# Streaming rows at 192 bytes into a block of 256: a change of SBUF places in a two-block model kernel

## The chip, the core and the metric

The kernel runs on one core of one Trainium2 chip. A core has TensorE (PE: matrix products into PSUM, with its weight loads listed apart as PEld), VectorE (DVE), ScalarE (ACT), GpSimd (POOL) and SyncE (SP, here the queue of the weight transfers), which share the on-chip memory SBUF of 128 partitions. The metric is device time in microseconds (us) of one execution; the times are of three runs, and one further execution was profiled.

## The reference, cut to what matters

Two model blocks are computed one after the other on 256 tokens and 16 meta tokens (T = 272 rows), in float32. The first is a mixer (state-space part and convolution) followed by PEER, a layer that picks 16 experts per head for each token:

```python
q = (xt @ w_query).reshape(t, PEER_HEADS, PEER_DKEY)
v1, i1 = lax.top_k(s1, PEER_TOPK)       # s1, s2: q against 128 sub-keys
...
act = jax.nn.gelu(jnp.einsum("td,thkd->thk", xb, u), approximate=False) * gb
return jnp.einsum("thk,thkd->td", act, v)
```

The second has two layers, each with a SwiGLU feed-forward (FFN), an attention, an output projection and another FFN:

```python
h = h + 0.5 * _swiglu(_rms_norm(h, ln_ffn1[layer]), ffn1_wi[layer], ffn1_wo[layer])
hn = _rms_norm(h, ln_mix[layer])
...
h = h + mix @ w_out[layer]
h = h + 0.5 * _swiglu(_rms_norm(h, ln_ffn2[layer]), ffn2_wi[layer], ffn2_wo[layer])
```

## The kernel before

**Products.** The state `h` lies transposed: 8 tiles (KD) of 128 features, each with 272 token columns. All large products go through `mm3`. A float32 value is split into a high part (fp32r, made by ACT) and the rest (made by DVE or POOL), for the weights (`wH`, `wL`, `_split`) and for the data (`uH`, `uL` and others, `hilo`). Each 128x128 weight tile then gives three matmuls, wH with xH, wH with xL, wL with xH. The weight tile is the stationary operand; the data row, 256 or 272 columns of one feature tile, streams. These streaming rows are what the change moves.

**Weights.** `_load` fetches 8 weight tiles (512 KB) at a time on SP's queue into one of three `raw` buffers. `_split` makes halves of 4 tiles into one of five `wH` and `wL` buffers. A split of `wL` is DVE's, except for the share that `self.share` hands to POOL.

**Stages, in order.** `mixer`; `peer`; then `second`: FFN1, attention A (`attn_a`), FFN2, FFN3, attention B (`attn_b`), FFN4. Every FFN has a first part, 44 output tiles of 8 products-of-three with `uH`/`uL` (its pairs), and a second part of 8 tiles of 22 products-of-three with the gate rows `gH`/`gL`. FFN4 and the output projection of attention B work on 256 columns, `peer` too; FFN1 to FFN3 and attention A on 272.

**PEER.** First 16 query tiles; then 128 value rows r, each one output tile (24 matmuls) followed by a Gelu (L957, L960). Meanwhile `route` finds the top 16 on DVE. From r = 60 on, each row carries one group g of four tokens: `onehot(g)` on DVE (L931) compares the 128 key numbers with the chosen ones (`sel`), for both halves of an expert number at once; every fourth group is multiplied by its gate values on DVE (L933), the others by four ACT instructions (L936); `gates(g)` multiplies the halves on PE (L943), and DVE and ACT write the result into `buf` (L945, L947). `onehot` writes one of two buffers, so it runs a group ahead. After the 128 rows, PE runs the `up` products: for each of 128 gate rows, split into `uH`/`uL` by `act`, 24 matmuls at L999.

**Places.** `uH` and `uL` are each one tile of 8 rows of 272 columns. A row is 1088 bytes, so the starts of successive rows step by 64 within a block of 256 bytes. A pass over columns 16 to 271 (`self.u(M, T)`) begins 64 bytes later in each row. The gate rows of the FFNs have a pitch of 512 columns (256 in FFN4), behind a filler tile `gpad`.

Of the kernel before, what the change touches and what calls it, by code (L numbers as in the profile page):

```python
# [8 lines left out]
F32 = mybir.dt.float32  # L9
# [9 lines left out]
P = 128  # L19
# [20 lines left out]
R0 = 271  # L40
RW = 400
# [166 lines left out]
class Net:  # L208
    def __init__(self, tc, ctx, I, out, dump=None):
# [29 lines left out]
        self.uH = per.tile([P, KD, T], F32R, name="uH")  # L239
        self.uL = per.tile([P, KD, T], F32R, name="uL")  # L240
# [139 lines left out]
    def u(self, a=0, b=T):  # L380
        return lambda k: (self.uH[:, k, a:b], self.uL[:, k, a:b])
# [5 lines left out]
    def norm_tile(self, d):  # L387
        nc, a, b = self.nc, self.na, self.nb
        src = self.h[:, d, a:b]
        self.hilo(self.uH[:, d, a:b], self.uL[:, d, a:b], src, self.vec(self.nw, d))  # L390
# [58 lines left out]
    def mixer(self):  # L449
        nc = self.nc  # L450
        h = self.h
        with ExitStack() as ctx:
# [8 lines left out]
            yH, yL = self.uH[:, :, M:], self.uL[:, :, M:]  # L461
# [5 lines left out]
            nH = pool.tile([P, KD, T], F32R, name="nH")  # L467
            nL = pool.tile([P, KD, T], F32R, name="nL")
# [152 lines left out]
            pool = ctx.enter_context(self.tc.tile_pool(name="my", bufs=1))  # L621
            cH = pool.tile([P, KD, S], F32R, name="cH")
# [173 lines left out]
    def peer(self):  # L796
# [5 lines left out]
        with ExitStack() as ctx:  # L802
# [3 lines left out]
            sel = pool.tile([P, S, 2], F32, name="sel")  # L806
            gsel = pool.tile([P, S], F32, name="gsel")
# [37 lines left out]
            self.linear(16, KD, self.u(M, T), S, qf)  # L845
            nc.scalar.dma_start(out=hd_, in_=h[:, :, M:])
            for d in range(KD):
                t = self.t_("t", 2)[:, :S]
                nc.vector.scalar_tensor_tensor(out=t, in0=h[:, d, M:], scalar=self.vec("norm_ffn", d), in1=r, op0=ALU.mult, op1=ALU.mult)
                self.hilo(self.uH[:, d, M:], self.uL[:, d, M:], t)  # L850
# [18 lines left out]
            def route(tt):  # L869
# [51 lines left out]
                nc.vector.tensor_copy(out=sel[:, ts].rearrange("p t i -> p i t"), in_=p2[:, :256].rearrange("p (i t) -> p i t", i=2))  # L921
# [42 lines left out]
            for r_ in range(NT):  # L964
                self.linear(1, KD, self.u(M, T), S, lambda m, ps: value(r_, ps))
# [60 lines left out]
            def u(d):  # L1026
                self.hilo(self.uH[:, d, M:], self.uL[:, d, M:], h[:, d, M:], w2[:, d : d + 1])
# [37 lines left out]
    def ffn(self, nxt, final=False, lo=0, each=None):  # L1065
        nc = self.nc
        with self.tc.tile_pool(name="ff", bufs=1) as pool:
# [3 lines left out]
            pool.tile([P, 112], F32, name="gpad")  # L1071
# [64 lines left out]
    def attn_a(self, nxt):  # L1136
        nc = self.nc
        with ExitStack() as ctx:
# [70 lines left out]
            oH = pool.tile([P, 8, T], F32R, name="oH")  # L1209
            oL = pool.tile([P, 8, T], F32R, name="oL")  # L1210
# [111 lines left out]
    def attn_b(self, nxt):  # L1322
        nc = self.nc
        with ExitStack() as ctx:
# [5 lines left out]
            qH = pool.tile([P, 2, T], F32R, name="qH")  # L1330
            qL = pool.tile([P, 2, T], F32R, name="qL")
# [3 lines left out]
            vt = pool.tile([P, 3, 1024], F32, name="vt")  # L1335
            oH = pool.tile([P, 8, S], F32R, name="oH")
# [173 lines left out]
    def second(self):  # L1510
        self.share = 0.0
        with self.tc.tile_pool(name="bp", bufs=1) as bp:
# [7 lines left out]
            with self.psum(3, 2, 3):  # L1520
                for l in range(2):
                    if l:
                        self.ffn("ln_mix_1")
# [5 lines left out]
                    self.ffn(None if l else "ln_ffn1_1", final=(l == 1), lo=M * l)  # L1529
# [57 lines left out]
```

## Time and profile before

| | before |
|---|---|
| median of 3 runs | 2240.27 us (2238.11 to 2245.38) |
| profiled execution, its own time | 2239.97 us |
| span of the profile, first to last instruction | 2238.0 us |
| PE busy, matmuls | 2169.0 us, 97% of the span, 17351 |
| DVE, ACT, POOL busy | 1590.4, 1323.0, 671.7 us |
| transfers | 356.59 MB, 159 GB/s |

A matmul's duration in the profile is that of one in a pipeline, about 0.28 us, while the next one starts some 0.12 us later. How fast PE goes through a stage is therefore read from the number of matmuls in a stretch of time, or from the distance of two starts, not from durations or from the busy share.

### The profile page before, as it was taken

Reading aid. Unit: us, or ns where it says so; the run is one execution under the profiler, and the core shown is the slowest. Engines: PE = TensorE matmul, PEld = TensorE weight load, DVE = VectorE, ACT = ScalarE, POOL = GpSimd, SP = SyncE. Lnnn points to the kernel's source line nnn. Section 1 sums busy time; section 2 is a strip of 40 time slices with the busy share of each in tenths; the row PEclk is TensorE's granted clock in tenths of the full one; section 3 lists DMA queues with packets and bytes.
Section 4 is the critical chain, followed back from the end, with each engine's and each line's share of the span. In section 5 each row is a group of like instructions: output and inputs, shape, how many; then the busy total and the mean of one; then the engine's idle time right before and its main releaser. Section 6 shows DMA issues by size and latency. Waiting matters only on the chain.

```text
span 2238.0 us, 45779 instructions
## 1 busy us (share of the span) xinstructions
PE 2169.0 (97%) x17351; PEld 2096.4 (94%) x17351; DVE 1590.4 (71%) x3143; ACT 1323.0 (59%) x2857; POOL 671.7 (30%) x567
## 2 busy tenths in 40 slices
PE   8998998899999999999999999999999999899999
PEld 7987998899999999999999998899999999679999
DVE  8889789955778766666586655876656666877664
ACT  8776654556766755555565555765555555666553
POOL 6684744444555400000031114122201211512220
PEclk9999999999999999999999999999999999999999
DMA  4523644454444555555565554145555555204555
GB/s 170 166 97 133 201 148 142 154 186 151 142 136 139 181 189 188 186 184 188 186 207 188 179 168 144 58 150 173 178 179 170 177 174 187 76 29 128 192 183 169
DMA packets 103948, 356.59 MB, mean 159 GB/s; under 512 B 12416, under 2 KB 20016, under 8 KB 103344
## 3 DMA queue, kind: packets, MB, share of 16 engines
q1 hardware_dynamic: 100096, 346.06, 46.8%
q10 hardware_dynamic: 3632, 7.62, 1.1%
q8 instruction: 136, 2.23, 0.4%
q14 instruction: 84, 0.69, 0.1%
HBM read 351.51 MB, written 5.40 MB: 159 GB/s over the span
## 4 chain that ended last, share of the span: by engine, by line
PE 76%; DVE 14%; ACT 5%; issue 3%; POOL 1%; DMA 1%; DVEq 0%; SPq 0%; ACTq 0%; POOLq 0%
PE acc L999 16%; PE mm L317 13%; PE mm L315 13%; PE mm L316 13%; PE acc L317 4%; PE acc L315 4%; PE acc L316 4%; DVE wL L294 3%; DVE h L931 2%; ACT h L936 1%; ACT wH L288 1%; DVE acc L526 1%; PE mm L1461 1%; PE acc L1485 1%; PE acc L943 1%
## 5 line engine op out<-in xcount | busy, mean ns | idle before, releaser
L288 ACT ACTIVATE wH<-raw 128x512 fp32r<-128x512 f32 x1296 | 806.6, 628 | 559.9 <-PE mm L316 237.8
L294 DVE TENSOR_TENSOR wL<-raw,wH 128x512 fp32r<-128x512 f32 x1037 | 756.3, 731 | 381.0 <-ACT wH L288 358.7
L317 PE MATMUL mm<-uH,wL 128*128 128x256 f32 (+1 forms) x2168 | 620.1, 286 | 19.9 <-DVE wL L294 19.2
L315 PE MATMUL mm<-uH,wH 128*128 128x256 f32 (+1 forms) x2168 | 628.3, 290 | 9.9 <-ACT wH L288 7.0
L316 PE MATMUL mm<-uL,wH 128*128 128x256 f32 (+1 forms) x2168 | 618.9, 286 | 2.4 <-DVE uL L359 2.3
L294 POOL TENSOR_TENSOR wL<-raw,wH 128x512 fp32r<-128x512 f32 x259 | 383.4, 1485 | 462.9 <-ACT wH L288 354.0
L317 PEld LDWEIGHTS mm<-uH,wL 128*128 128x128 f32 x2168 | 411.0, 190 | 24.7 <-DVE wL L294 23.8
L315 PEld LDWEIGHTS mm<-uH,wH 128*128 128x128 f32 x2168 | 410.9, 190 | 15.5 <-ACT wH L288 8.7
L316 PEld LDWEIGHTS mm<-uL,wH 128*128 128x128 f32 x2168 | 410.7, 189 | 5.9 <-DVE uL L359 4.2
L999 PE MATMUL acc<-uH,wH 128*128 128x256 f32 x1024 | 288.4, 282 | 1.7 <-DVE h L1033 1.1
L999 PE MATMUL acc<-uL,wH 128*128 128x256 f32 x1024 | 287.7, 281 | 0.4 <-DVE uL L357 0.4
L999 PE MATMUL acc<-uH,wL 128*128 128x256 f32 x1024 | 287.2, 281 | 0.0
L1086 POOL TENSOR_TENSOR t<-t,g 128x272 f32<-128x272 f32 (+1 forms) x88 | 108.2, 1231 | 415.6 <-ACT wH L288 326.2
L317 PE MATMUL acc<-uH,wL 128*128 128x272 f32 (+1 forms) x728 | 209.4, 288 | 0.0
L315 PE MATMUL acc<-uH,wH 128*128 128x272 f32 (+1 forms) x728 | 209.1, 287 | 0.0
L316 PE MATMUL acc<-uL,wH 128*128 128x272 f32 (+1 forms) x728 | 208.7, 287 | 0.0
L317 PE MATMUL mm<-gH,wL 128*128 128x272 f32 (+1 forms) x704 | 199.9, 284 | 0.0
L315 PE MATMUL mm<-gH,wH 128*128 128x272 f32 (+1 forms) x704 | 199.9, 284 | 0.0
L316 PE MATMUL mm<-gL,wH 128*128 128x272 f32 (+1 forms) x704 | 199.8, 284 | 0.0
L999 PEld LDWEIGHTS acc<-uH,wH 128*128 128x128 f32 x1024 | 194.1, 190 | 2.5 <-DVE h L1033 1.5
L999 PEld LDWEIGHTS acc<-uL,wH 128*128 128x128 f32 x1024 | 193.1, 189 | 0.6 <-DVE uL L357 0.6
L999 PEld LDWEIGHTS acc<-uH,wL 128*128 128x128 f32 x1024 | 193.0, 189 | 0.0
(400 smaller groups left out, 3918.0 us busy)
## 6 DMA issues: line engine op xcount, KB each, us to landing
raw<-in_wall_dram SPq DMA_DIRECT2D x648, 512.0 KB, 3.3
bdram<-brow ACTq DMA_DIRECT2D x1, 3200.0 KB, 13.7
b<-bdram SPq DMA_DIRECT2D x8, 272.0 KB, 4.6
b<-bdram SPq DMA_DIRECT2D x8, 144.0 KB, 4.2
buf<-in_keys_dram ACTq DMA_DIRECT2D x1, 1024.0 KB, 6.4
hd<-h ACTq DMA_DIRECT2D x1, 1024.0 KB, 5.4
h<-hd ACTq DMA_DIRECT2D x1, 1024.0 KB, 6.4
uv<-in_uv_dram ACTq DMA_DIRECT2D x1, 1024.0 KB, 5.8
```

The costliest lines, as they stand in the source:

```text
L288: nc.scalar.activation(out=H, in_=w, func=AF.Copy)
L294: eng.tensor_tensor(out=L, in0=w, in1=H.bitcast(F32), op=ALU.subtract)
L315: mm(ps, H, xH, start=(k == 0), stop=False)
L316: mm(ps, H, xL, start=False, stop=False)
L317: mm(ps, L, xH, start=False, stop=(k == kt - 1))
L526: nc.vector.scalar_tensor_tensor(out=acc, in0=src, scalar=w, in1=acc, op0=ALU.mult, op1=ALU.add)
L931: nc.vector.tensor_tensor(out=o, in0=self.iota[:, None, None, :].to_broadcast([P, 4, 2, P]), in1=sel[:, ts, :, None].to_broadcast([P, 4, 2 ...
L936: nc.scalar.activation(out=o[:, t, 0], in_=o[:, t, 0], func=AF.Copy, scale=gsel[:, 4 * g + t : 4 * g + t + 1])
L943: nc.tensor.matmul(ps[:, :, t], o[:, t, 1], o[:, t, 0], start=True, stop=True)
L999: nc.tensor.matmul(o, a, b, start=(r == 0 and d % 2 == 0 and i == 0), stop=(r == NT - 1 and i == 2), skip_group_check=True)
L1086: nc.gpsimd.tensor_tensor(out=t, in0=t, in1=s, op=ALU.mult)
L1461: nc.tensor.matmul(ps[:, :nk], qa[hh][:, k, a : a + n], ckv[:, k, :nk], start=(k == 0), stop=(k == 1))
```

## The change

It gives places in SBUF to the rows that stream. In the diff (cut):

```diff
+PITCH = 320
+AT = 64
+NPAD = 64
+OPAD = 80
+QPAD = 112
+EPAD = 112
+GPADS = (336, 432, 400, 432)
...
-        self.uH = per.tile([P, KD, T], F32R, name="uH")
-        self.uL = per.tile([P, KD, T], F32R, name="uL")
+        per.tile([P, 48], F32, name="upad")
+        u = [per.tile([P, KD * PITCH], F32R, name=n) for n in ("uH", "uL")]
+        per.tile([P, 80], F32, name="wpad")
+        self.uH, self.uL = (t.rearrange("p (k c) -> p k c", c=PITCH) for t in u)
+        self.vH, self.vL = (t[:, : KD * S].rearrange("p (k c) -> p k c", c=S) for t in u)
...
     def u(self, a=0, b=T):
+        if a == M and b == T:
+            return lambda k: (self.vH[:, k], self.vL[:, k])
         return lambda k: (self.uH[:, k, a:b], self.uL[:, k, a:b])
...
-            nH = pool.tile([P, KD, T], F32R, name="nH")
-            nL = pool.tile([P, KD, T], F32R, name="nL")
+            pool.tile([P, NPAD], F32, name="npad")
+            nH = pool.tile([P, KD, PITCH], F32R, name="nH")[:, :, :T]
+            nL = pool.tile([P, KD, PITCH], F32R, name="nL")[:, :, :T]
...
+            pool.tile([P, 112], F32, name="cpad")
             cH = pool.tile([P, KD, S], F32R, name="cH")
...
-            sel = pool.tile([P, S, 2], F32, name="sel")
-            gsel = pool.tile([P, S], F32, name="gsel")
+            sel = [self.t_("g", 2)[:, :S] for _ in range(2)]
+            gsel = self.t_("ssq", 2)[:, :S]
...
-                nc.vector.tensor_tensor(out=o, in0=self.iota[:, None, None, :].to_broadcast([P, 4, 2, P]), in1=sel[:, ts, :, None].to_broadcast([P, 4, 2, P]), op=ALU.is_equal)
+                for i in range(2):
+                    nc.vector.tensor_tensor(out=o[:, :, i], in0=self.iota[:, None, :].to_broadcast([P, 4, P]), in1=sel[i][:, ts, None].to_broadcast([P, 4, P]), op=ALU.is_equal)
...
-                t = self.uH[:, i, M:], self.uL[:, i, M:]
+                t = self.uH[:, i, AT:], self.uL[:, i, AT:]
...
-            pool.tile([P, 112], F32, name="gpad")
+            pool.tile([P, pad], F32, name="gpad")
...
+            pool.tile([P, EPAD], F32, name="epad")
             oH = pool.tile([P, 8, S], F32R, name="oH")
```

`oH`/`oL` of attention A and `qH`/`qL` of attention B get a filler and the pitch of 320 columns in the same way as `nH`. The tables `sel` and `gsel`, which had tiles of their own, move into scratch buffers, which makes room.

The addresses of the two built programs give these places (bytes into a block of 256 at which the rows that stream start; "all" means 0, 64, 128 and 192 in turn). Weight tiles start at a multiple of 512 in both programs.

| rows, columns | matmuls | place before | place after | from a high row to its low row, modulo 1024: before, after |
|---|---|---|---|---|
| u, 272 | 3984 | all | 192 | 512, 0 |
| u in queries, values, w_out of the mixer, FFN4, 256 | 4704 | all | 192 | 512, 0 |
| u at L999, 256 | 3072 | one of the four for 24 matmuls | 192 | 512, 0 |
| n (mixer), 272 and 256 | 696 and 192 | all and all | 192 and 0 | 512, 0 |
| o of attention A, q of attention B, 272 | 192 and 216 | all | 192 | 512 (o), 128 (q); 0 |
| c (mixer), 256 | 192 | 192 | 128 | 0, 0 |
| o of attention B, 256 | 192 | 192 | 64 | 0, 0 |
| g of FFN1 and FFN3, 272 | 1056 | 192 | 64 | 0, 0 |
| g of FFN2, 272, and FFN4, 256 | 528 and 528 | 192 | 192 | 0, 0 |

PE's instructions stand in the same order as before. On DVE, POOL and ACT the order changes in `peer` alone. DVE, at groups 25 to 28 of the gates, before (L945 writes the products into `buf`, L931 is `onehot`, L933 its multiplication, L294 a weight split, L961 a Gelu product):

```order
749 L945 TENSOR_TENSOR buf<-acc,buf 128x85x4
750 L931 TENSOR_TENSOR h<-cst,sel 128x1024
751 L945 TENSOR_TENSOR buf<-acc,buf 128x86x4
752 L294 TENSOR_TENSOR wL<-raw,wH 128x512
753 L931 TENSOR_TENSOR h<-cst,sel 128x1024
754 L961 TENSOR_TENSOR buf<-t,buf 128x100
755 L945 TENSOR_TENSOR buf<-acc,buf 128x87x4
756 L931 TENSOR_TENSOR h<-cst,sel 128x1024
757 L294 TENSOR_TENSOR wL<-raw,wH 128x512
```

And DVE at the same place after (L963, L949, L304, L979 are those lines now):

```order
757 L963 TENSOR_TENSOR buf<-acc,buf 128x85x4
758 L949 TENSOR_TENSOR h<-cst,g 128x4x128 x2
759 L963 TENSOR_TENSOR buf<-acc,buf 128x86x4
760 L304 TENSOR_TENSOR wL<-raw,wH 128x512
761 L949 TENSOR_TENSOR h<-cst,g 128x4x128 x2
762 L979 TENSOR_TENSOR buf<-t,buf 128x100
763 L963 TENSOR_TENSOR buf<-acc,buf 128x87x4
764 L304 TENSOR_TENSOR wL<-raw,wH 128x512
765 L949 TENSOR_TENSOR h<-cst,g 128x4x128 x2
```

One comparison of 1024 elements has become two of 512, and one weight split stands ahead of the comparison that it followed.

ACT at groups 21 to 22 of the gates before (L936 scales one of four blocks by its gate, L957 and L960 are the Gelu, L288 a weight split, L947 a copy of the products):

```order
612 L288 ACTIVATE wH<-raw 128x512
613 L936 ACTIVATE h<-h,gsel 128x128 x3
614 L957 ACTIVATE buf<-mm 128x160
615 L960 ACTIVATE t<-mm 128x96
616 L936 ACTIVATE h<-h,gsel 128x128
617 L288 ACTIVATE wH<-raw 128x512
618 L947 ACTIVATE buf<-acc 128x42x4
```

And ACT at the same place after:

```order
602 L298 ACTIVATE wH<-raw 128x512
603 L954 ACTIVATE h<-h,ssq 128x128 x4
604 L975 ACTIVATE buf<-mm 128x160
605 L978 ACTIVATE t<-mm 128x96
606 L298 ACTIVATE wH<-raw 128x512
607 L965 ACTIVATE buf<-acc 128x42x4
```

The four scalings of a group now stand together ahead of the Gelu. By the built program they wait for the first of the two comparisons alone, since it writes the blocks that they scale.

## Rows read from the trace of the kernel before

**Rows 1.** The page: busy time by engine, and the chain that ended last by engine.

```profile
PE 2169.0 (97%) x17351; PEld 2096.4 (94%) x17351; DVE 1590.4 (71%) x3143; ACT 1323.0 (59%) x2857; POOL 671.7 (30%) x567
...
PE 76%; DVE 14%; ACT 5%; issue 3%; POOL 1%; DMA 1%; DVEq 0%; SPq 0%; ACTq 0%; POOLq 0%
```

**Rows 2.** Stretches: us; PE, PEld, DVE, ACT, POOL busy (count); clock, DMA share, GB/s.

```profile
455.00:515.00 60.00, 58.38 (x493) 58.18 (x494) 24.16 (x36) 30.99 (x62) 27.95 (x21) 1.00 0.57 185
770.00:1120.00 350.00, 350.00 (x2957) 349.87 (x2956) 212.86 (x373) 195.43 (x374) 0.00 (x0) 1.00 0.57 186
2055.00:2170.00 115.00, 115.00 (x973) 114.95 (x972) 80.12 (x145) 65.60 (x125) 24.34 (x21) 1.00 0.57 186
```

**Rows 3.** PE in order of time (start us, duration us): FFN4's gate rows, 256 columns.

```profile
2190.03 0.28 PE L315 MATMUL mm<-gH,wH 128*128 128x256 f32 x1
...
2191.05 0.28 PE L315 MATMUL mm<-gH,wH 128*128 128x256 f32 x1
```

**Rows 4.** PE in order of time: FFN2's pairs, then its gate rows, 272 columns.

```profile
1559.74 0.29 PE L315 MATMUL mm<-uH,wH 128*128 128x272 f32 x1
...
1562.01 0.29 PE L315 MATMUL acc<-uH,wH 128*128 128x272 f32 x1
...
1639.86 0.29 PE L315 MATMUL mm<-gH,wH 128*128 128x272 f32 x1
...
1642.08 0.29 PE L315 MATMUL mm<-gH,wH 128*128 128x272 f32 x1
```

**Rows 5.** PE at L999: the first matmuls of five successive gate rows.

```profile
877.92 0.28 PE L999 MATMUL acc<-uH,wH 128*128 128x256 f32 x1
...
880.75 0.28 PE L999 MATMUL acc<-uH,wH 128*128 128x256 f32 x1
...
883.60 0.28 PE L999 MATMUL acc<-uH,wH 128*128 128x256 f32 x1
...
886.42 0.28 PE L999 MATMUL acc<-uH,wH 128*128 128x256 f32 x1
...
889.30 0.28 PE L999 MATMUL acc<-uH,wH 128*128 128x256 f32 x1
```

**Rows 6.** The stretch of the top-16 search, columns as in rows 2.

```profile
300.00:450.00 150.00, 131.71 (x1048) 127.30 (x1047) 146.20 (x436) 74.70 (x148) 67.24 (x44) 0.98 0.44 145
```

**Rows 7.** DVE, ACT and POOL in order of time, gate groups 28 to 32.

```profile
617.06 1.22 DVE L931 TENSOR_TENSOR h<-cst,sel 128x1024 f32<-128x1024 f32 x1
...
621.12 1.21 DVE L931 TENSOR_TENSOR h<-cst,sel 128x1024 f32<-128x1024 f32 x1
623.62 0.53 DVE L945 TENSOR_TENSOR buf<-acc,buf 128x360 f32<-128x360 f32 x1 [1.29 <-ACT buf L957]
...
632.34 1.22 DVE L931 TENSOR_TENSOR h<-cst,sel 128x1024 f32<-128x1024 f32 x1
...
622.43 0.99 ACT L936 ACTIVATE h<-h,gsel 128x128 f32<-128x128 f32 x3 [0.38 <-DVE h L931]
...
617.19 2.24 POOL L294 TENSOR_TENSOR wL<-raw,wH 128x512 fp32r<-128x512 f32 x1 [0.86 <-DVE wL L294]
```

**Rows 8.** PE in order of time: the gate products of groups 4, 5 and 44.

```profile
531.42 1.05 PE L943 MATMUL acc<-h 128*128 128x128 f32 x8
535.15 1.05 PE L943 MATMUL acc<-h 128*128 128x128 f32 x8
...
681.53 1.16 PE L943 MATMUL acc<-h 128*128 128x128 f32 x8 [0.19 <-DVE h L933]
```

**Rows 9.** L931 and L933: count, ns (min/median/max), first and last start in us.

```profile
L931 DVE TENSOR_TENSOR h<-cst,sel x64: 1205/1217/1498, 411.9 to 750.6; 128x1024 f32<-128x1024 f32 x64
...
L933 DVE TENSOR_TENSOR h<-h,gsel x16: 671/1666/1780, 422.0 to 740.1; 128x512 f32<-128x512 f32 x16
```

**Rows 10.** DVE in order of time: the multiplication that readies gate group 4.

```profile
527.19 1.77 DVE L933 TENSOR_TENSOR h<-h,gsel 128x512 f32<-128x512 f32 x1
```

**Rows 11.** A stretch of the mixer, PE alone: us, busy (count), clock, DMA share, GB/s.

```profile
30.00:140.00 110.00, 104.25 (x781) 0.98 0.42 135
```

More of the change, by code (lines that the diff above doesn't have):

```diff
@@ L389, in norm_tile @@
         src = self.h[:, d, a:b]
-        self.hilo(self.uH[:, d, a:b], self.uL[:, d, a:b], src, self.vec(self.nw, d))
+        self.hilo(*self.u(a, b)(d), src, self.vec(self.nw, d))
         if d == 0:
@@ L460, in mixer @@
             cy = pool.tile([P, KD, S], F32, name="cy")
-            yH, yL = self.uH[:, :, M:], self.uL[:, :, M:]
+            yH, yL = self.vH, self.vL
             xs = pool.tile([P, 16, T], F32, name="xs")
@@ L843, in qf @@
                 self.later.append((0, scores))
-            self.linear(16, KD, self.u(M, T), S, qf)
+            self.linear(16, KD, self.u(M), S, qf)
             nc.scalar.dma_start(out=hd_, in_=h[:, :, M:])
@@ L849, in peer @@
                 nc.vector.scalar_tensor_tensor(out=t, in0=h[:, d, M:], scalar=self.vec("norm_ffn", d), in1=r, op0=ALU.mult, op1=ALU.mult)
-                self.hilo(self.uH[:, d, M:], self.uL[:, d, M:], t)
+                xH, xL = self.u(M)(d)
+                self.hilo(xH, xL, t)
             v = carve(8, 2, 16)
@@ L920, in route @@
                 nc.tensor.transpose(p2[:, 256:384], tv.rearrange("p h j -> p (h j)"), self.ident)
-                nc.vector.tensor_copy(out=sel[:, ts].rearrange("p t i -> p i t"), in_=p2[:, :256].rearrange("p (i t) -> p i t", i=2))
+                for i in range(2):
+                    nc.vector.tensor_copy(out=sel[i][:, ts], in_=p2[:, i * P : (i + 1) * P])
                 nc.vector.tensor_copy(out=gsel[:, ts], in_=p2[:, 256:384])
@@ L930, in onehot @@
                 ts = slice(4 * g, 4 * g + 4)
-                nc.vector.tensor_tensor(out=o, in0=self.iota[:, None, None, :].to_broadcast([P, 4, 2, P]), in1=sel[:, ts, :, None].to_broadcast([P, 4, 2, P]), op=ALU.is_equal)
+                for i in range(2):
+                    nc.vector.tensor_tensor(out=o[:, :, i], in0=self.iota[:, None, :].to_broadcast([P, 4, P]), in1=sel[i][:, ts, None].to_broadcast([P, 4, P]), op=ALU.is_equal)
                 if g % 4 == 0:
@@ L964, in peer @@
             for r_ in range(NT):
-                self.linear(1, KD, self.u(M, T), S, lambda m, ps: value(r_, ps))
+                self.linear(1, KD, self.u(M), S, lambda m, ps: value(r_, ps))
                 pace += 1.5
@@ L1026, in u @@
             def u(d):
-                self.hilo(self.uH[:, d, M:], self.uL[:, d, M:], h[:, d, M:], w2[:, d : d + 1])
+                self.hilo(self.uH[:, d, M:T], self.uL[:, d, M:T], h[:, d, M:], w2[:, d : d + 1])
             for d in range(KD):
@@ L1062, in peer, with ffn @@
             self.factor = factor
-    def ffn(self, nxt, final=False, lo=0, each=None):
+    def ffn(self, nxt, final=False, lo=0, each=None, pad=GPADS[0]):
         nc = self.nc
@@ L1208, in attn_a @@
             rq = self.token_root(pool, pq, 16, 1.0 / 64, 0.125)
-            oH = pool.tile([P, 8, T], F32R, name="oH")
-            oL = pool.tile([P, 8, T], F32R, name="oL")
+            pool.tile([P, OPAD], F32, name="opad")
+            oH = pool.tile([P, 8, PITCH], F32R, name="oH")[:, :, :T]
+            oL = pool.tile([P, 8, PITCH], F32R, name="oL")[:, :, :T]
             def tail(items):
@@ L1329, in attn_b @@
             cq = pool.tile([P, 2, T], F32, name="cq")
-            qH = pool.tile([P, 2, T], F32R, name="qH")
-            qL = pool.tile([P, 2, T], F32R, name="qL")
+            pool.tile([P, QPAD], F32, name="qpad")
+            qH = pool.tile([P, 2, PITCH], F32R, name="qH")[:, :, :T]
+            qL = pool.tile([P, 2, PITCH], F32R, name="qL")[:, :, :T]
             kix = pool.tile([P, 2, T], F32, name="kix")
@@ L1522, in second @@
                     if l:
-                        self.ffn("ln_mix_1")
+                        self.ffn("ln_mix_1", pad=GPADS[2])
                         self.dump("h1a", self.h)
@@ L1528, in second @@
                     self.dump(f"h{l}b", self.h)
-                    self.ffn(None if l else "ln_ffn1_1", final=(l == 1), lo=M * l)
+                    self.ffn(None if l else "ln_ffn1_1", final=(l == 1), lo=M * l, pad=GPADS[1 + 2 * l])
                     self.dump(f"h{l}c", self.h)
```

## The prediction

> **What bounds the kernel now.** I read the page first, the chain by engine, then the stretches of each stage, then single starts. PE is busy for 97% of the span and takes 76% of the chain that ended last [rows 1]: the rate at which PE issues matmuls is the first thing to look at. Busy time hides it, because matmuls overlap, so I divide stretches by counts. At L999, 350 us hold 2957 matmuls, 118.4 ns each, with PE never idle and the granted clock at 1.00; FFN4's pairs need 115 / 973 = 118.2 ns [rows 2]. FFN4's second part, with the same 256 columns and the same weight tiles, does nine in 1.02 us, 113.3 ns [rows 3]. With 272 columns the same holds: FFN2's pairs do 18 in 2.27 us, 126.1 ns, its gate rows 18 in 2.22 us, 123.3 ns [rows 4]. So at one clock and one size, PE streams some rows 5 ns and others 3 ns faster, with no wait in between.
>
> What differs is where rows lie, by the table of places: the gate rows all start at 192 of 256, with the low row at the same place modulo 1024 as the high row; the others take all four places, with the low row 512 further. L999 is a natural experiment, since each gate row r stays at one place for 24 matmuls. Five starts [rows 5] give 2.83, 2.85, 2.82 and 2.88 us for rows at 64, 128, 192 and 0, that is 117.9, 118.8, 117.5 and 120.0 ns. Place matters, but a row at 192 alone does not reach 113.3. What is left of what that row lacks is the equal place of high and low row, which the change gives too. I take both together to be what makes a stream fast; that is an inference, and its failure is a rival below.
>
> Two stretches are not PE's. During the top-16 search DVE is busy for 146.2 of 150 us [rows 6], so a faster PE only waits longer there. In the gate stage of PEER (about 520 to 754 us) PE looks full, but something else sets the pace. Four groups, from one `onehot` start at 617.06 to another at 632.34, take 15.28 us, 3.82 us a group [rows 7], while PE's own row is 535.15 - 531.42 = 3.73 us [rows 8]. Group 4 is ready at 527.19 + 1.77 = 528.96 us [rows 10], 2.46 us before PE comes to it; at group 44 PE waits for DVE [rows 8]. So DVE and ACT start ahead, lose about 0.07 us per group, and are caught by group 40. Their loop is what sets the end: L931, then ACT's scaling, then the Gelu behind it, which DVE's L945 waits for with 1.29 us of idle time [rows 7].
>
> **The change part by part.**
>
> L999: 3072 matmuls from 118.4 to 113.3 ns, 15.7 us. DVE and ACT are at 61% and 56% there and DMA at 0.57 [rows 2], so they can follow.
>
> FFN4's pairs: 1056 matmuls from 118.2 to 113.3, 5.2 us. Their rows get a pitch of 1024 bytes and equal places, as FFN4's gate rows have.
>
> FFN1 to FFN3, pairs: 3168 matmuls with 272 columns. Their rows keep a step of 1280 bytes, 256 modulo 1024 from one row to the next, which no row here shows. The bounds are 123.3 (as gate rows) and 126.1 (nothing). I take 124.0, near the first since the place in the block is the same: 2.1 ns each, 6.7 us. Bounds 0 and 8.9.
>
> Queries and values, 3456 matmuls, by stretch. The PE-bound rows from 455 to about 520 us run at 60 / 493 = 121.7 ns with some waits [rows 2]; the 384 matmuls of the queries take 47 us at that rate. 4.2% (5 of 118.4) of these 112 us is 4.7. The search gives nothing. The gate stage gives nothing as far as its loop of DVE and ACT stays as it is. The last three rows give 0.4. Sum 5.1.
>
> The halved `onehot`: a comparison of 1024 elements takes 1217 ns [rows 9], so one of 512 takes about 610 plus what an instruction costs to start. The nearest row of that size, L933 at its shortest, is 671 ns; two are 1342, 0.13 us more per group, 8 us over 64 groups, on DVE. Against it, ACT no longer waits for the second half: its scaling starts after some 0.67 instead of 1.22 us in three groups of four, which shortens the loop by up to 0.55 us there. What can eat this: L933 takes 1666 ns in the median where POOL splits weights beside it, and POOL's split that starts at 617.19 in L931's time takes 2.24 us [rows 7, 9]; they hold each other up. Between two halves POOL can now slip in, about 1.0 us (1666 - 671), though in every fourth group it is then out of L933's way. Bounds per group: -0.4 and +1.0 us. I take 0, since the gain and the loss are of one size and the second half has slack (ACT's four scalings last 4 x 0.33 us beside it).
>
> On this pair of engines the Trainium skill (SBUF — State Buffer, section "SBUF: two separate sides") says that a DVE instruction with two SBUF inputs and a GpSimd instruction that reads SBUF lock each other out, whole instruction by whole instruction. The trace agrees, with the 671 and 1666 ns of L933; the rule would let POOL in at every seam that the halving makes.
>
> Small ones. Mixer rows n, 696 with 272 columns: 110 us hold 781 matmuls, 141 ns each [rows 11], so waits are mixed in; half of 2.1 ns, 0.7. Mixer's w_out, 192 with 256 columns, 5 ns: 0.9. Attention A's keys and queries (384) and o (192), the start and attention B's entry (240), 2.1 ns: 1.7. Together 3.3.
>
> Losses. Rows c go from 192 to 128 and o of attention B from 192 to 64, 384 matmuls. By L999's rows at those places [rows 5] they would fall from 113.3 to 118.8 and 117.9: 1.9 us. Nothing is the other bound, since their high and low rows stay equal. I take 1.9. Mixer rows n with 256 columns go to 0, at worst 120.0 against 118.4: 0.3. The gate rows of FFN1 and FFN3 go from 192 to 64, 1056 matmuls: at L999 those two places are 0.4 ns apart [rows 5], so I take nothing; bounds +2.9 us (back to 126.1) and -2.9.
>
> Sum: 15.7 + 5.2 + 6.7 + 5.1 + 3.3 - 1.9 - 0.3 = 33.8 us off the profiled execution's 2239.97 (span 2238.0 and 2 us around it), 2206.2; that execution is 0.3 us from the median of 2240.27, so **2206 us**.
>
> **The rivals.**
>
> *Place is not it at L999* (0.13). The row at 192 there ran at 117.5, and L999 also differs from the fast stages in writing eight accumulators in turn. If that costs the 4 ns, L999 saves only 3072 x 0.9 = 2.8 instead of 15.7: 2219 us. For it: rows 5. Against it: the value rows, which write one bank, are as slow as L999, 121.7 ns with waits [rows 2].
>
> *The place does nothing* (0.04). The fast stages could be fast for something else, such as that nothing else writes near them; then only the halved `onehot` acts: about 2240. For it: the row at 192. Against it: FFN2's two parts, 126.1 and 123.3, with the same engines at work [rows 4].
>
> The Trainium skill (TensorE: Matmul & The Clock Gate, section "Back-to-back issue gap") has this as its rule: at full clock a matmul follows another after columns / 2.4 plus 2.5 ns, which is an estimate of 109.2 and 115.8 ns here, wherever its operands lie. By it nothing would change, 2240; by the rows the sum stands at 2206. The trace differs: four values from 117.5 to 120.0 at one size and clock.
>
> *The gate stage gets longer* (0.11). If POOL's turn at the seam falls on the loop, each group takes up to 1.0 us more. A third of that, 0.33 x 60 = 20 us, gives 2226 (0.07). From 0.56 us per group on (33.8 / 60) nothing is left of the gain; at 1.0 in all 60 groups it is 60 us, **2266, slower than before** (0.04). For it: L933's 1666 ns. Against it: the second half isn't waited for by ACT.
>
> *More* (0.07): the loop shortens by 0.2 us per group and 272 columns reach 123.3, -12 and -2: 2192.
>
> **How the numbers follow.** The forecast's own case has 0.65, with bounds of 2196 (8.9 for 6.7, no loss at c and o, 0.1 us per group off the loop) and 2214 (272 columns give nothing). Leaving out the slow gate stage, most of *More* and the case without effect, the range is 2194 to 2220 us; it holds the first case, L999's rival and part of *More*, about 0.8. What a measurement can tell is 0.3%, 7 us. Faster by more: 0.65 + 0.13 + 0.07 + 0.07 = 0.92; same 0.04; slower 0.04.
>
> **What would show it.** L999 in 348 instead of 364 us, with starts 113 ns apart and one value for all four rows; FFN4's pairs near 113; FFN pairs near 124; the search unchanged at 150 us; onehot halves of about 0.67 us, and 3.8 us from group to group in the gate stage, with PE waiting there earlier than group 40. I am wrong if L999 keeps 117 to 118 ns, or if L931's successors are seen with a second half of over 1.5 us and groups over 4.2 us apart.

## The result, and the profile after

The changed kernel takes 2215.93 us (median of 4 runs, 2213.64 to 2219.34) against 2240.45 us of the kernel before beside it (2238.11 to 2245.38): ratio 0.9891, 95% interval 0.9878 to 0.9905. That is 24.5 us less, where 34 were forecast. The profiled execution has a span of 2211.8 us. The page of the kernel after, busy time by engine and the chain that ended last by engine:

```profile
PE 2141.8 (97%) x17351; PEld 2068.6 (94%) x17351; DVE 1616.4 (73%) x3209; ACT 1318.9 (60%) x2857; POOL 658.7 (30%) x567
...
PE 79%; DVE 13%; ACT 3%; issue 3%; POOL 1%; DMA 1%; SPq 0%; DVEq 0%; ACTq 0%; POOLq 0%
```

Beside [rows 1] PE bounds the kernel as before, with the same matmuls in 27 us less of busy time. Where the 26.2 us of span come from is seen stage by stage. The table gives the time from the first matmul of a stage to the first of the next, worked out from PE's starts in the trace. `again` and `again2` are two more profiled executions of the changed kernel (experiments 1 and 9):

| stage, us | forecast of the change | before | after | `again` | `again2` |
|---|---|---|---|---|---|
| up to the first matmul | | 6.3 | 6.1 | 6.9 | 6.8 |
| mixer | 1.1 less with attention | 251.1 | 248.4 | 250.5 | 250.7 |
| PEER up to L1017 | 5.1 less | 505.9 | 501.9 | 503.5 | 503.6 |
| L1017 (L999 before) | 15.7 less | 367.1 | 351.8 | 352.4 | 351.8 |
| pairs of FFN1, FFN2, FFN3 | 6.7 less | 402.9 | 394.8 | 395.7 | 394.8 |
| gate rows of FFN1, FFN3 | 0 | 131.0 | 134.6 | 134.6 | 134.6 |
| gate rows of FFN2 | 0 | 65.1 | 65.1 | 65.1 | 65.1 |
| attention A and B, with o | see mixer | 319.7 | 318.8 | 321.8 | 321.8 |
| pairs of FFN4 | 5.2 less | 125.4 | 124.8 | 120.1 | 124.8 |
| gate rows of FFN4, to the end | 0 | 63.3 | 65.6 | 63.3 | 65.6 |
| span | 33.8 less | 2238.0 | 2211.8 | 2213.8 | 2219.7 |

L1017 came out as forecast. In the kernel after, PE in order of time, the first matmuls of four successive gate rows start 2.72 us apart, 24 matmuls each, so 113.3 ns. There is one value for all rows where [rows 5] had four:

```profile
876.92 0.28 PE L1017 MATMUL acc<-uH,wH 128*128 128x256 f32 x1
...
879.64 0.28 PE L1017 MATMUL acc<-uH,wH 128*128 128x256 f32 x1
...
882.36 0.28 PE L1017 MATMUL acc<-uH,wH 128*128 128x256 f32 x1
...
885.08 0.28 PE L1017 MATMUL acc<-uH,wH 128*128 128x256 f32 x1
```

FFN4 did not. Stretches of the kernel after, PE alone (us, busy and count of matmuls, two of which overlap the ends, clock, DMA share, GB/s): L1017, FFN4's pairs and its gate rows, FFN2's pairs and FFN1's gate rows.

```profile
780.00:1090.00 310.00, 310.00 (x2738) 1.00 0.58 194
2030.00:2140.00 110.00, 110.00 (x936) 1.00 0.54 184
2150.00:2200.00 50.00, 50.00 (x427) 1.00 0.59 195
1480.00:1580.00 100.00, 100.00 (x813) 1.00 0.52 178
1250.00:1300.00 50.00, 50.00 (x397) 1.00 0.50 172
```

110 / 934 is 117.8 ns in FFN4's pairs, the forecast's 113.3 missed, although all these rows start at 192. Its gate rows, 113.3 ns before [rows 3], are at 50 / 425 = 117.6 now, although they still start at 192. FFN1's gate rows, which moved to 64, take 50 / 395 = 126.6 instead of 123.3. FFN2's pairs reach 123.3, better than the 124.0 that was taken.

In the gate stage these four groups keep about the pace of the forecast. In the kernel after, DVE and ACT in order of time (start, duration, idle time before in brackets), groups of the same four-group turn as [rows 7]:

```profile
615.10 1.28 DVE L949 TENSOR_TENSOR h<-cst,g 128x512 f32<-128x512 f32 x2
617.40 0.53 DVE L963 TENSOR_TENSOR buf<-acc,buf 128x360 f32<-128x360 f32 x1 [1.02 <-ACT buf L975]
...
618.74 2.38 DVE L949 TENSOR_TENSOR h<-cst,g 128x512 f32<-128x512 f32 x2
...
630.10 1.27 DVE L949 TENSOR_TENSOR h<-cst,g 128x512 f32<-128x512 f32 x2
```

Four groups take 15.0 us, 3.75 each (3.82 before). Two comparisons of 512 take 1.28 us together; one alone takes 684 ns in the median. Where POOL splits weights beside them (its split starts at 618.86), the second half grows, so that two last 2.38 us. That is the seam of the rival. Here PE does not wait for it, but late in the stage it does: at group 48 such a pair of 2.38 us stands ahead of the multiplication (L951) for which PE then waits 0.52 us (PE's idle time in the trace). From group 48 on PE waits at every fourth group, 1.1 us in all. The sign that PE would wait earlier than group 40 did not come.

The stage as a whole, the 64 rows that carry a group, took 237.2 us where the kernel before took 239.5, a gain that the forecast had put at nothing.

### The profile page after: what moved, and what is told of

It is laid out like the page before. It is cut to its first block, busy times and chain, and to the rows that moved or that the text cites. A ratio compares the mean times of both kernels' runs of the same rounds, so it can differ in the third digit from the quotient of the medians.

```text
span 2211.8 us, 45890 instructions
## 1 busy us (share of the span) xinstructions
PE 2141.8 (97%) x17351; PEld 2068.6 (94%) x17351; DVE 1616.4 (73%) x3209; ACT 1318.9 (60%) x2857; POOL 658.7 (30%) x567
## 4 chain that ended last, share of the span: by engine, by line
PE 79%; DVE 13%; ACT 3%; issue 3%; POOL 1%; DMA 1%; SPq 0%; DVEq 0%; ACTq 0%; POOLq 0%
PE acc L1017 15%; PE mm L327 14%; PE mm L325 14%; PE mm L326 14%; PE acc L327 4%; PE acc L326 4%; PE acc L325 4%; DVE wL L304 3%; DVE h L949 1%; PE acc L961 1%; DVE acc L540 1%; PE mm L1482 1%; PE acc L1506 1%; ACT wH L298 1%; POOL wL L304 1%
## 5 line engine op out<-in xcount | busy, mean ns | idle before, releaser
L304 DVE TENSOR_TENSOR wL<-raw,wH 128x512 fp32r<-128x512 f32 x1037 | 751.3, 726 | 366.5 <-ACT wH L298 350.9
L304 POOL TENSOR_TENSOR wL<-raw,wH 128x512 fp32r<-128x512 f32 x259 | 371.6, 1440 | 466.3 <-ACT wH L298 366.3
L1017 PE MATMUL acc<-uH,wH 128*128 128x256 f32 x1024 | 283.1, 277 | 1.2 <-DVE h L1051 1.1
L1017 PE MATMUL acc<-uL,wH 128*128 128x256 f32 x1024 | 282.8, 276 | 0.3 <-DVE uL L367 0.3
L1017 PE MATMUL acc<-uH,wL 128*128 128x256 f32 x1024 | 282.2, 276 | 0.0
L325 PE MATMUL mm<-gH,wH 128*128 128x272 f32 (+1 forms) x704 | 201.6, 286 | 0.0
L326 PE MATMUL mm<-gL,wH 128*128 128x272 f32 (+1 forms) x704 | 201.6, 286 | 0.0
L327 PE MATMUL mm<-gH,wL 128*128 128x272 f32 (+1 forms) x704 | 201.6, 286 | 0.0
L1017 PEld LDWEIGHTS acc<-uH,wH 128*128 128x128 f32 x1024 | 192.2, 188 | 1.7 <-DVE h L1051 1.6
L1017 PEld LDWEIGHTS acc<-uL,wH 128*128 128x128 f32 x1024 | 192.2, 188 | 0.5 <-DVE uL L367 0.5
L1017 PEld LDWEIGHTS acc<-uH,wL 128*128 128x128 f32 x1024 | 192.0, 188 | 0.0
```

Source lines behind the costliest of these rows:

```text
L304: eng.tensor_tensor(out=L, in0=w, in1=H.bitcast(F32), op=ALU.subtract)
L325: mm(ps, H, xH, start=(k == 0), stop=False)
L326: mm(ps, H, xL, start=False, stop=False)
L327: mm(ps, L, xH, start=False, stop=(k == kt - 1))
L1017: nc.tensor.matmul(o, a, b, start=(r == 0 and d % 2 == 0 and i == 0), stop=(r == NT - 1 and i == 2), skip_group_check=True)
```

## The experiments

Theory after the result: place is not all. A stream at 192 has **two rates**, 113.3 and 117.8 ns (123.3 and 126.7 with 272 columns). It holds one until it is broken, and what starts it again picks the next. Rival 1: FFN4's rows are slow themselves, all at one place modulo 1024. Rival 2: FFN4 takes its rate over from the stage ahead of it, whose rows (o of attention B) went to 64. Still open from the prediction: whether the low row must share the high row's place, and what the halved comparison does.

**1. `again`: the changed kernel, unchanged.**

> The changed kernel once more, to see whether the rates of its stages are fixed. In its first profile FFN4 kept 117.8 ns a matmul in pairs and gate rows although its rows start at 192, while L1017 kept 113.3. Theory (a stream at 192 has two rates, 113.3 and 117.8 ns; which one holds is set when PE starts again after a wait, and lasts until the next): with the same waits at the same places FFN4 comes out at 117.8 again, or at 113.3 if a wait ended a little differently; nothing in between. Rival (FFN4's rows, all at one place modulo 1024, are slower than the four rows of L1017): 117.8 in every execution. Time 2216 us, 7 us less if FFN4 is seen at 113.3.

2217.1 us (2213.02 to 2219.24). FFN4 ran at the fast rate in this execution of the same program. PE in its pairs and gate rows:

```profile
2040.00:2140.00 100.00, 100.00 (x885) 1.00 0.60 193
2155.00:2205.00 50.00, 50.00 (x443) 1.00 0.61 196
```

100 / 883 and 50 / 441 are 113.3 ns. Rival 1 falls: the same rows at the same places have both rates. Rival 2 falls as a rule too, since o ran at 117.8 ns here as well.

**2. `all192`: the places that the change had moved off 192.**

```diff
-EPAD = 112
-GPADS = (336, 432, 400, 432)
+EPAD = 80
+GPADS = (432, 432, 432, 432)
...
-            pool.tile([P, 112], F32, name="cpad")
+            pool.tile([P, 128], F32, name="cpad")
```

> Rows c of the mixer, o of attention B and the gate rows of FFN1 and FFN3 go to 192 too (fillers changed); FFN4's rows stay where they are. If place sets the rates: gate rows of FFN1 and FFN3 from 126.7 to 123.3 ns (1056 matmuls, 3.5 us), c from 118.7 to 113.3 and o from 117.8 to 113.3 (384 matmuls, 1.9 us), FFN4 unchanged at 117.8: 5.4 us off 2216, so 2210.5. If FFN4 inherits its rate from the stage ahead of it (o at 117.8, handed on without a wait long enough to change it): o at 113.3 makes FFN4's pairs and gate rows 113.3 too, 1584 matmuls by 4.45 ns, 7.0 us more: 2203.5.

2207.23 us (2205.76 to 2212.66), ratio to before 0.9856 (0.9831 to 0.9882); that lies between the two forecasts, 2210.5 and 2203.5. FFN1's gate rows, FFN4's pairs and its gate rows, PE:

```profile
1250.00:1300.00 50.00, 50.00 (x408) 1.00 0.56 182
2030.00:2140.00 110.00, 110.00 (x973) 1.00 0.59 192
2145.00:2195.00 50.00, 50.00 (x443) 1.00 0.62 196
```

The gate rows of FFN1 and FFN3 are back at 123.3 ns (50 / 406 = 123.2), 65.9 and 65.1 us as before the change. FFN4 is fast. What the places of these gate rows cost, 3.6 us, is settled by this; what made FFN4 fast is not, since `again` was fast without it. A share of o's place in it is neither shown nor excluded.

**3. `nudge`: the stream of FFN4 broken five times.**

```diff
+            if self.nudge and m % 4 == 3:
+                self.nc.tensor.transpose(self.bank("ax")[:, :P], self.cst[:, :P], self.ident)
             evac(m, a, b)
```

> The changed kernel with one added transpose of 128 columns on PE after every fourth pair of FFN4 (pairs 4, 8, 12, 16, 20); its result is not used. It only breaks the stream for about 0.2 us, five times 0.2 us = 1 us. Theory of two rates: FFN4's stretches between the transposes come out at 113.3 or 117.8 ns, each constant until the next transpose, and some of them at 113.3; four pairs are 192 matmuls, 0.85 us less for each stretch at 113.3, and the gate rows (528, 2.35 us) keep what the last stretch had. Rival (FFN4's rows are slow themselves): 117.8 in all stretches and 1 us more in time.

2213.74 us (2210.85 to 2216.92). Stretches ahead of the first transpose and between the five:

```profile
2036.00:2049.00 13.00, 13.00 (x117) 1.00 0.48 161
2051.00:2072.00 21.00, 21.00 (x181) 1.00 0.62 193
2074.00:2094.00 20.00, 20.00 (x179) 1.00 0.56 184
2096.00:2116.00 20.00, 20.00 (x179) 1.00 0.57 188
2118.00:2138.00 20.00, 20.00 (x172) 1.00 0.56 183
```

Without the two at the ends these are 113.0, 117.3, 113.0, 113.0 and 117.6 ns: fast, slow, fast, fast, slow, with nothing in between and a change only at a break. Behind the fifth transpose the last pairs are fast again, and the gate rows keep that, as expected (63.3 us). This shows the two rates directly.

**4. `scan`: other places, and low rows elsewhere than high rows.**

```diff
-                t = self.uH[:, i, AT:], self.uL[:, i, AT:]
+                a = 8 * (r % 8) if r < 80 else AT
+                j = i if r < 40 or r >= N0 else (i + 2) % LAST if r < 80 else (i + 1) % LAST if r < 112 else i
+                t = self.uH[:, i, a : a + S], self.uL[:, j, a : a + S]
```

> The products after PEER's rows (L1017) with other places for the streaming rows: gate rows 0 to 39 start at 192, 224, 0, 32, 64, 96, 128, 160 of 256 in turn, low row at the same place modulo 1024; rows 40 to 79 the same places with the low row 512 further; rows 80 to 111 at 192 with the low row 256 further; rows 112 on as in the changed kernel. What is computed stays the same. If place alone sets the rate: 113.3 ns at 192, about 117.8 at 64, 118.7 at 128, 120.0 at 0, and the same in rows 40 to 79. If the equal place of high and low row is needed as well: rows 40 to 111 at 192 run at about 117.5 (as the row at 192 did before the change), only rows 0 to 39 and 112 on reach 113.3. If place does nothing and the phase after a wait does it all: one rate over rows 0 to 79, whatever the place.

(Against the last sentence of that text, the rows that start ahead of 64 columns overwrite the first 16 columns of FFN1's input here too, so the output differs; the same work is timed.) Starts of the rows at 192, 224, 0, 32, 64, 96, 128, 160 and 192 with equal places; then, after the dots, of a row at 192 and the next with the low row 512 further:

```profile
803.29 0.28 PE L1019 MATMUL acc<-uH,wH 128*128 128x256 f32 x1
...
806.01 0.28 PE L1019 MATMUL acc<-uH,wH 128*128 128x256 f32 x1
...
808.85 0.28 PE L1019 MATMUL acc<-uH,wH 128*128 128x256 f32 x1
...
811.72 0.28 PE L1019 MATMUL acc<-uH,wH 128*128 128x256 f32 x1
...
814.55 0.28 PE L1019 MATMUL acc<-uH,wH 128*128 128x256 f32 x1
...
817.39 0.28 PE L1019 MATMUL acc<-uH,wH 128*128 128x256 f32 x1
...
820.25 0.28 PE L1019 MATMUL acc<-uH,wH 128*128 128x256 f32 x1
...
823.10 0.28 PE L1019 MATMUL acc<-uH,wH 128*128 128x256 f32 x1
...
825.92 0.28 PE L1019 MATMUL acc<-uH,wH 128*128 128x256 f32 x1
...
916.45 0.28 PE L1019 MATMUL acc<-uH,wH 128*128 128x256 f32 x1
...
919.18 0.28 PE L1019 MATMUL acc<-uH,wH 128*128 128x256 f32 x1
```

A row at 192 takes 2.72 us, the seven others 2.82 to 2.87 (117.5 to 119.6 ns), 0 the longest. With the low row 512 further 192 takes 2.73, the same; rows 80 to 111, 256 further, keep 113.3. So the equal place of high and low row, on which the prediction's inference stood, does nothing. (The table of places gives 0 for q of attention B after the change; two rows of 1280 bytes lie between its high and low rows, which is 512 modulo 1024.)

**5. `halved`: the kernel before with the halved comparison alone.**

```diff
-            sel = pool.tile([P, S, 2], F32, name="sel")
-            gsel = pool.tile([P, S], F32, name="gsel")
+            sel = [self.t_("g", 2)[:, :S] for _ in range(2)]
+            gsel = self.t_("ssq", 2)[:, :S]
```

and the two comparisons and two copies of the change with it.

> The kernel before with one part of the change alone: the comparison in halves, with its tables in scratch buffers; all rows keep their old places. The prediction took nothing for it (bounds -0.4 to +1.0 us for each of 64 groups): 2240 us, PEER up to L999 in 505.9 us as before. Rival: the halving carries part of the 4.0 us that PEER lost in the changed kernel's profile (505.9 to 501.9): 2236 to 2238 us, and then the places have less to do with it. The other rival of the prediction, POOL let in at the seam, would show as more than 2240.

2237.81 us (2235.86 to 2242.52) against 2240.16, ratio 0.999 (0.998 to 1.0); PEER up to L999 took 504.5 us in its profile. It gives 0 to 4.5 us, about 2 at the median, so the times alone do not exclude that it gives nothing. PE's starts say where: the 64 rows of the gate stage took 238.0 us instead of 239.5 and the four rows behind them 12.4 instead of 13.1, with all but the last groups 3.73 us apart, where the kernel before had gaps of up to 4.08 from group 39 on. So the forecast's nothing was about 2 us too low, by one profile of each kernel, and neither bound of that term was near.

**6. `shiftw`: every weight tile 64 bytes further.**

```diff
-        per.tile([P, 80], F32, name="wpad")
+        per.tile([P, 96], F32, name="wpad")
```

> The changed kernel with every weight tile 64 bytes further (at 64 of 512); the rows at L1017, in the queries, values and FFN pairs stay at 192, those of the later stages move by 64 with the weights. Theory 1 (the row's own place counts): L1017 stays at 113.3 ns. Theory 2 (the distance between row and weight tile counts): L1017 takes the value of a row at 128, 118.8 ns, 16.4 us more there.

**12. `bothshift`: rows and weight tiles 64 bytes further** (`upad` of 64 columns for 48).

> The changed kernel with every streaming row and every weight tile 64 bytes further (rows at 0 of 256, weight tiles at 64 of 512). If the distance from weight tile to row counts, each stage keeps the rate of the changed kernel: L1017 at 113.3 ns, 352 us from its first to its last matmul. If the row's own place counted as well, L1017 would run at 120.0 ns as a row at 0 did, 20 us longer.

L1017 in `shiftw`, then in `bothshift`, PE:

```profile
780.00:1090.00 310.00, 310.00 (x2615) 1.00 0.57 186
```

```profile
780.00:1090.00 310.00, 310.00 (x2738) 1.00 0.61 194
```

With the weights alone moved, rows at 192 run at 310 / 2613 = 118.6 ns, the value of a row at 128 (the stage takes 368.0 us for 351.8), and one execution took 2247.61 us. With rows at 0 and weights at 64 they run at 113.3 (352.0 us; one execution took 2216.55). What counts, by this one shift of 64 bytes, is the distance from weight tile to row, not the row's place; the kernel before and the change could not show it, since all weight tiles lie at multiples of 512 in both. FFN4's pairs, moved to a distance of 128 by `shiftw`, PE:

```profile
2070.00:2170.00 100.00, 100.00 (x835) 1.00 0.58 184
```

That is 100 / 833 = 120.0 ns, where L1017 has 118.6 at the same distance: a distance of 128 does not have one single rate either.

**7. `scan2`: the order of the places, and finer ones.**

```diff
+                a = AT
+                if r < 32:
+                    a = (32, 48, AT, 16)[r % 4]
+                elif r < 64:
+                    a = (56, AT, 60, AT, 4, AT, 58, 2)[r % 8]
+                elif r < 96:
+                    a = (48, AT, 32, AT, 16, AT, 8, AT)[r % 8]
```

> L1017 with other places again, high and low row equal. Rows 0 to 31 go 64, 128, 192, 0 of 256 in turn, as L999 did before the change. Rows 32 to 63 go 160, 192, 176, 192, 208, 192, 168, 200, rows 64 to 95 go 128, 192, 64, 192, 0, 192, 224, 192; rows 96 on stay at 192. It leaves the first 16 columns of FFN1's input overwritten by rows that start ahead of them, so the output is not the reference's. Theory (two rates at 192, taken over from what ran ahead): the rows at 192 that follow one at 128 run at 117.5 to 117.8, as before the change, and those that follow 160 at 113.6, as in the scan. Rival (the kernel before was slow at 192 for another reason, such as its low row 512 further): all rows at 192 run at 113.3 to 113.7. Places from 168 to 208 lie between 113.3 and 118 if the fast place is broad, and at 117 to 118 beside a single 192 if it is narrow.

Starts of rows at 128, 192, 0 in the order of the kernel before; then at 168, 200, 160; then at 128, 192, 64, 192, 0:

```profile
787.39 0.28 PE L1024 MATMUL acc<-uH,wH 128*128 128x256 f32 x1
...
790.24 0.28 PE L1024 MATMUL acc<-uH,wH 128*128 128x256 f32 x1
...
793.06 0.28 PE L1024 MATMUL acc<-uH,wH 128*128 128x256 f32 x1
...
869.54 0.28 PE L1024 MATMUL acc<-uH,wH 128*128 128x256 f32 x1
...
872.42 0.28 PE L1024 MATMUL acc<-uH,wH 128*128 128x256 f32 x1
...
875.33 0.28 PE L1024 MATMUL acc<-uH,wH 128*128 128x256 f32 x1
...
965.25 0.28 PE L1024 MATMUL acc<-uH,wH 128*128 128x256 f32 x1
...
968.10 0.28 PE L1024 MATMUL acc<-uH,wH 128*128 128x256 f32 x1
...
970.92 0.28 PE L1024 MATMUL acc<-uH,wH 128*128 128x256 f32 x1
...
973.75 0.28 PE L1024 MATMUL acc<-uH,wH 128*128 128x256 f32 x1
...
976.48 0.28 PE L1024 MATMUL acc<-uH,wH 128*128 128x256 f32 x1
```

In the old order the row at 192 takes 2.82 us: this is the slow one of [rows 5], now with its low row at the equal place. After a row at 128 it takes 2.82 (968.10), after one at 64 2.73 (973.75). So which rate a row at 192 has depends on the rows ahead of it. The row just ahead does not settle it alone: three rows at 192 behind one at 128 (gate rows 2 and 6, in the first two turns of the places, and 65, in the first turn of its own order) took 2.73, 2.72 and 2.74 us, and all others behind one at 128 are slow. The trace of the kernel before has the same. Its gate row 2, at 192 behind one at 128 and with its low row 512 further, starts and ends thus:

```profile
769.88 0.28 PE L999 MATMUL acc<-uH,wH 128*128 128x256 f32 x1
...
772.60 0.28 PE L999 MATMUL acc<-uH,wH 128*128 128x256 f32 x1
```

That is 2.72 us, 113.3 ns; row 6 took 2.72 too, and from row 10 on every row at 192 took 2.83. So the trace before already held rows that were fast without the equal place. The fast place is narrow: 2.86 us at 176 and at 208, 2.88 at 168 and 2.91 at 200, no better than the other multiples of 32.

**8. `nudges`: which break leaves which rate.** Before the first matmul of each gate row at L1017 (in rows 60 to 79 before its second):

```diff
+                w = 32 if kind == 4 else P
+                for _ in range((1, 2, 3, 1, 1, 4)[kind]):
+                    nc.tensor.transpose(self.bank("ax")[:w, :P], self.cst[:, :w], self.ident)
```

> The changed kernel with added transposes on PE at the start of each of 124 gate rows at L1017, results not used: 1 in rows 0 to 19, 2 in rows 20 to 39, 3 in 40 to 59, 1 between the first and second matmul of the row in 60 to 79, 1 with 32 columns in 80 to 99, 4 in 100 to 119, none after. It shows which rate a stream takes when it starts again. If it is chance: both rates in every block of 20 rows, without order. If the kind of break decides: one rate per block, or a strict turn of the two in a block, as in the queries, where one search product stands between two query tiles. Each row at 117.8 instead of 113.3 is 0.11 us.

2269.82 us in one execution, L1017 402.7 us. Starts of successive rows, first with one transpose, then with two:

```profile
792.95 0.37 PE L1026 MATMUL acc<-uH,wH 128*128 128x256 f32 x1
...
795.80 0.36 PE L1026 MATMUL acc<-uH,wH 128*128 128x256 f32 x1
...
798.74 0.36 PE L1026 MATMUL acc<-uH,wH 128*128 128x256 f32 x1
...
822.03 0.36 PE L1026 MATMUL acc<-uH,wH 128*128 128x256 f32 x1
...
825.16 0.36 PE L1026 MATMUL acc<-uH,wH 128*128 128x256 f32 x1
...
828.28 0.36 PE L1026 MATMUL acc<-uH,wH 128*128 128x256 f32 x1
```

With one transpose rows take 2.85 or 2.94 us, and of the 60 rows of the three such blocks 21 are slow (6, 7 and 8 of 20). In the first two blocks they come in no strict turn; in the third, with 32 columns, rows 84 to 99 go two slow, two fast throughout. With two, three or four the products of all 60 rows start 113 ns apart. So it is neither of the two answers alone: one break leaves both rates possible, by a turn or without one; several in a row left the fast rate here.

**9 to 11. `again2`, `all192b` and `guard`, side by side.** `guard` is `all192b` with

```diff
+                    if final:
+                        p = self.bank("ax")
+                        for _ in range(2):
+                            nc.tensor.transpose(p[:, :P], self.cst[:, :P], self.ident)
```

> The changed kernel a third time, beside the two runs below. Theory (one break in the stream leaves the rate to chance): its executions spread over some 7 us, by whether FFN4's 1584 matmuls take 113.3 or 117.8 ns, about 2213 to 2220 us, median 2216. Rival (a fixed rate for every stage): all within 3 us.

> The kernel with rows c, o of attention B and the gate rows of FFN1 and FFN3 at 192 too, again, now side by side with the changed kernel. By the stages 5.4 us less (gate rows 3.6, c and o 1.8), 2211, and what FFN4's chance adds or takes: 2207 to 2214. If the places of these 1440 matmuls did nothing: 2216.

> The kernel all192b with two transposes on PE after the first pair of FFN4, right behind the norm's product, results not used. Since two transposes in a row left the fast rate in all 20 rows at L1017, FFN4's pairs and gate rows take 113.3 ns in every execution: 0.6 us more for the transposes, up to 7 us less in executions that would have had the slow rate, so 2207 and a narrower spread. Rival (the choice at L1017 doesn't carry over to FFN4): 2212, as all192b plus 0.6, and its profile may show 117.8.

| | median, us | lowest to highest | ratio to before (95%) | FFN4 in its profile |
|---|---|---|---|---|
| `again2` | 2217.91 | 2211.62 to 2221.53 | 0.9886 (0.9867 to 0.9905) | 117.8 |
| `all192b` | 2207.52 | 2204.68 to 2212.09 | 0.9856 (0.9836 to 0.9875) | 113.3 |
| `guard` | 2209.64 | 2202.53 to 2211.90 | 0.9851 (0.9831 to 0.9871) | 113.3 |

FFN4's pairs in `again2`, then in `guard`:

```profile
2040.00:2140.00 100.00, 100.00 (x851) 1.00 0.58 190
```

```profile
2035.00:2140.00 105.00, 105.00 (x929) 1.00 0.59 194
```

The medians of `again2` and `all192b` lie inside the spans that were expected; single executions lie up to 2.4 us outside. `all192` is the best version, 10 us under the changed kernel in both comparisons (2207.23 to 2217.1, 2207.52 to 2217.91). The guard adds nothing that these runs can tell: FFN4 was fast in all three profiles with o at 192, with and without the guard, and the spread of 9.4 us is no narrower. The narrower spread that was expected did not come. The rest of the spread is in stages that FFN4 does not touch: among the executions profiled here the mixer differs by 2 us, PEER by 4, each attention by 1.7.

## Why the prediction was right, and where it was wrong

The time lies in the stated range, partly by luck: the forecast's own case ended at 2214 us, and the range went on to 2220 for a rival at L999 that did not come.

The direction, the bound (PE's rate of issue, at one clock) and the largest term held: 15.7 us were forecast at L999 and 15.3, 14.7 and 15.3 came. The rival "place is not it at L999" is refuted, and so is "the place does nothing". That L999 has eight accumulators costs nothing that these rows show. By the formula of the Trainium skill that the prediction weighed (TensorE: Matmul & The Clock Gate, section "Back-to-back issue gap") a matmul's distance hangs on its columns alone, an estimate of 109.2 ns here. The section gives it for the isolated gap and says that in a stream with weight loads the loads count too, which the prediction left out. The runs show 113.3 to 121.2 ns at 256 columns by place, with the granted clock at 1.00 in the stretches above, and 113.3 and 117.8 at one place, so the traces do not follow the formula.

**The step that failed** is the inference that "both together", place and equal place, "make a stream fast". Equal place is not needed (experiment 4), and the right place does not suffice (experiments 1 and 3). The row at 192 in [rows 5], from which it was drawn, was simply at the slow rate, and two rows at 192 earlier in the same trace were not (experiment 7). L999 came out as forecast all the same, as the change also ended the turn of places there, with which `scan2` brought the slow rate back. Three terms were missed:

- FFN4's pairs, 5.2 us forecast: 0.6 or 5.3 by execution. Seven profiled executions have the start of FFN4 and the attention ahead of it as the change left them: `again` and `scan2` were fast (120.1 us), and so was `nudge` up to its first transpose; after, `again2`, `scan` and `nudges` were slow (124.8). With 4 of 7 slow the term is worth about 2.6 us, an estimate from these.
- FFN4's gate rows, taken as unchanged: they take over the pairs' rate, 2.3 us lost in the slow executions.
- Queries and PE-bound values, 5.1 us forecast: PEER lost 4.0, 2.4 and 2.3, and mostly elsewhere. By PE's starts, before, after, `again` and `again2`: the 16 query tiles took 53.0, 52.2, 52.2 and 52.2 us, the 60 rows up to the gate stage 200.3, 200.0, 201.6 and 201.5, the gate stage 239.5, 237.2, 237.3 and 237.4, the last four rows 13.1 and three times 12.4. So of 4.7 us some 0.8 came in the queries, and nothing that can be told from the spread in the rows behind them; 2.2 came in the gate stage, put at 0, and 0.7 in the last rows. `halved` shows about 2 of these 2.9 without the places (experiment 5). A product of the search or of the gates stands between two rows and breaks the stream: in the profile after, successive query tiles run at 113.3 and 117.8 ns in turn, and gate groups up to the 40th come 3.63 and 3.72 us apart in turn (3.73 before).

**Terms mis-sized with the mechanism right.** The gate rows of FFN1 and FFN3 at 64: 0 was taken from L999's 0.4 ns between those two places, which compared 64 with a 192 at its slow rate; 3.6 us were lost, above the bound of 2.9. The pairs of FFN1 to FFN3: 6.7 taken, 7.2 to 8.1 came, near the other bound of 8.9. Rows c and o: 1.9 taken, 0.4 to 0.9 and 0.7 by the time from their first matmul to the next stage's, though their matmuls ran at 118.7 and 117.8 ns, near the 118.8 and 117.9 of the forecast: about 1.1 to 1.6 in all. The small terms of the mixer and attention (3.3) cannot be told from the 1 to 3 us by which these stages differ between executions. The search was as forecast, DVE-bound.

The sum with these: 15.3 + 0.6 + 8.1 - 3.6 - 2.3 + 4.0, 2.7 in the mixer, 0.9 in attention and 0.2 ahead of it make 25.9, the profile's 26.2 but for rounding. Against the forecast's 33.8 this profile lacks 7.6 us, which are, but for rounding, 6.9 in FFN4, 3.6 in the gate rows at 64, 1.1 in PEER and 0.4 at L1017, less 1.4 that the pairs of FFN1 to FFN3 gave beyond the forecast and 2.7 that the mixer, attention and start did. The timed median lacks 9.3; how the other executions behind it divide is not known, since only some were profiled.

The gate stage's rivals did not come: it got shorter, and POOL at the seam, which stretches a second half to 1.79 us at most, cost PE at most about 1 us late in the stage. The Trainium skill (SBUF — State Buffer, section "SBUF: two separate sides") has a DVE instruction with two SBUF inputs and a GpSimd instruction that reads SBUF lock each other out. The trace agrees: the same comparison took 684 ns in the median and up to 1787 ns beside a split of POOL.

## What to carry to other kernels

Where PE is the bound and streams without waits, divide its matmuls by time in every stage; 4% between stages of one shape at one clock is worth a look at where the rows lie relative to the weight tiles, and every row of the kernel wants the good distance, those that were already there too. An inference from one natural experiment should be tried on its order as well: the row at 192 was slow in the turn of places in which it stood, and the same trace had it fast at the start of the stage. A rate that holds for a thousand matmuls may have been picked by the last break in the stream, so a stage's rate wants more than one profile before it is a property of its rows.

## What the runs showed of the hardware

- The rate of a stream of 128x256 products depends on the distance from weight tile to row, modulo 256 bytes: 113.3 ns at 192, 117.5 to 119.6 at the other multiples of 32 in `scan`, 121.2 at 200 (2.91 us / 24). One row at 64 ran at 113.3 as well, the first behind the wait ahead of L1017 in `scan2`, so 192 may not be the only place with a fast rate. The same distance at addresses 64 bytes further gives the same rate at L1017 (`bothshift`).
- At 192 a stream has two rates, 113.3 and 117.8 ns (123.3 and 126.7 with 272 columns: FFN3's pairs in `bothshift` took 134.1 us instead of 130.7). That 192 is not alone in this is seen at 128, with 118.6 and 120.0 ns in `shiftw`. Which one holds can differ between executions of one program and lasted through 1500 matmuls.
- Two to four transposes in a row left the fast rate in 60 of 60 rows, one left the slow rate in 21 of 60; 16 of these 60 rows went in a strict turn, two slow and two fast.
- Open: what in the restart picks the rate, and why these distances differ. Neither was tried.
